# Reading out every other product of a seven-product matrix stage two clock steps later

## The chip, the cores and the metric

The kernel runs on one core of one Trainium2 chip. Its time is the device time of one execution in microseconds; three timed executions gave 789.0, 789.12 and 790.51, and the median, 789.12 us, is the time before. One more execution was profiled. That one took 790.67 us, of which 788.9 us are the span that the profiler shows, from the first to the last instruction. PE is TensorE (its matmuls; PEld are its weight loads), DVE is VectorE, ACT is ScalarE, POOL is GpSimd and SP issues the transfers.

## The reference, cut to what matters

One layer of a streaming encoder is computed for 512 prompt tokens and 64 sample tokens, 576 in all, with a model width of 1024 and a hidden width of 4096: an input projection, two kinds of attention, an output projection with a layer norm, a feed-forward part with a layer norm, and a gate. The change lies in the feed-forward part, in the product with `w_up`:

```python
hid = jnp.square(jax.nn.relu(jnp.einsum('bld,df->blf', x, w_up)))
x = layer_norm(ALPHA * x + jnp.einsum('blf,fd->bld', hid, w_down), ln2_g, ln2_b)
```

Everything is float32 in the reference.

## The kernel before, in words

**Precision.** Each float32 operand is held as two halves, a rounded high part and the rest (`BH`/`BL` for the layer's input, the two parts of a `whl` tile for a weight). One product of a weight block with an activation block is three matmuls: high times high, high times low, low times high. Weights arrive by DMA in `wraw` tiles; ACT casts the high part (line 183) and DVE subtracts it for the low part (line 187). The `whl` tiles form a ring, and a cast into one waits until PE has used what was in it.

**The feed-forward part.** The hidden width is cut into eight groups of 512. For each group there is an up stage, which fills `hid[g]`, and a down stage, which adds `hid[g]` times a block of `w_down` to `Y`. The order is U0, U1, D0, U2, D1, U3, ... D5, U7, and then the last two downs together with the second layer norm. `hid` has two buffers, `hidE` for even and `hidO` for odd groups, so a `hid[g]` is used a whole down stage after it has been filled.

**The seven-product stage.** U0 and U1 are plain. U2 to U7 (`up_sums`, lines 1319 to 1356) compute a two-by-two block product with seven block products in place of eight. Tokens are halved (A: 288, B: 288) and the width of 1024 is halved; sums of the weight blocks (line 210, into `wsum` or over `wraw`) and sums of the input blocks (`SX`, named `s` in the profile, made once ahead) feed the products. A group has two such pairs (`pair(0)` and `pair(1)`), each of seven products; a product is four width blocks times three matmuls, 12 matmuls of 128x128 by 128x288. So a stage has 2 x 7 x 12 = 168 matmuls, and a down stage has 8 x 2 x 12 = 192 of the same shape.

**Where products land.** PSUM has eight banks here: three tiles `g` of two banks each, used in turn (`psum_g`, line 1082), and two one-bank tiles `n` (`psum_n`). In a pair, products 0 and 1 go into the two banks of one `g` tile, 2 and 3 into those of the next, 4 and 5 into the third, and 6 into an `n` tile. Each product is then read out once or twice, by the short functions in `steps`:

- product 0: line 1330, ACT copies it to `u[0]`
- product 1: line 1331, DVE, `r[0] = ps + u[0]`
- product 2: line 1332, DVE, `u[1] = ps + u[0]`
- product 3: line 1333, DVE, `u[2] = ps + u[1]`
- product 4: line 1334, DVE, `r[1] = ps + u[2]`, and then `r[0:2]` goes through ReLU, square, cast and subtraction (lines 1349 to 1352) into `hid[g]`
- product 5: line 1335, DVE twice, `r[3]` and `r[2]`
- product 6: line 1336, DVE, `r[2]`, and then `r[2:4]` goes the same way into `hid[g]`

`u` has one buffer, `r` has two.

**What sets the order.** The kernel is written as a generator that yields after every six matmuls (`yield_every=6` in `gemm`, line 273), so a product is two steps. `drive` (line 89) advances `clock` by one at each yield, then runs up to three due entries of a queue. `later(delay, fn)` (line 71) puts `fn` into that queue, due at the clock of the call plus `delay`. A read-out with delay 0, put in after the second yield of its product, is thus written into the program after the first six matmuls of the next product. A scheduling layer then makes one stream of instructions for each engine out of what was written, in which it may let an instruction pass others that aren't ready, and puts semaphore waits where one engine needs another. On the chip each engine's stream runs in its order.

Of the kernel before, what the change touches and what calls it, by code (L numbers as in the profile page):

```python
# [10 lines left out]
AF = mybir.ActivationFunctionType  # L11
OP = mybir.AluOpType
# [24 lines left out]
def tile_hybrid_step(ctx: ExitStack, tc: tile.TileContext, I, O):  # L37
    nc = tc.nc
    PE, ACT, DVE, POOL, SP = nc.tensor, nc.scalar, nc.vector, nc.gpsimd, nc.sync
# [4 lines left out]
    def f(ap):  # L44
        return ap.bitcast(F32)
# [25 lines left out]
    def later(delay, fn):  # L71
        evq.append((clock[0] + delay, len(evq), fn))
# [200 lines left out]
    def gemm(ps, W, kmap, aH, aL, cols, yield_every=6, first=True, last=True, wc=slice(0, 128), k0=0):  # L273

        n = len(kmap) * 3
        i = 0
        for kw, ka in enumerate(kmap, k0):
            for w, a in ((0, aH), (0, aL), (1, aH)):
                PE.matmul(ps, W(w, kw, wc), a[:, ka, cols], start=(first and i == 0), stop=(last and i == n - 1))  # L279
                i += 1  # L280
                if i % yield_every == 0:
                    yield 1
# [799 lines left out]
    def psum_g():  # L1082
        turn[0] += 1
        if turn[0] % 3 == 2:
            return psB.tile([128, 2, 512], F32, name="g", tag="g", bufs=1)
        return psM.tile([128, 2, 512], F32, name="g", tag="m", bufs=2)

    def psum_n():
        return psN.tile([128, 512], F32, name="n", tag="n", bufs=2)
# [229 lines left out]
    def up_sums(g):  # L1319

        hid[g] = base.tile([128, 2, 4, NT], F32R, name="hidE", tag="AL") if g % 2 == 0 else \
            fb.tile([128, 2, 4, NT], F32R, name="hidO", tag="hidO")
        x11, x12, x22 = [[t[:, 4 * k:4 * k + 4, (A, B)[h]] for t in (BH, BL)] for h, k in ((0, 0), (0, 1), (1, 1))]
        def pair(m):
            h0 = WT.items[U["P", g, m]]["h0"]
            r = fs.tile([128, 4, HW], F32, name="r", bufs=2)
            u = fs.tile([128, 3, HW], F32, name="u")
            tt = DVE.tensor_tensor

            steps = ((x11, lambda ps: ACT.copy(u[:, 0], ps)),  # L1330
                     (x12, lambda ps: tt(r[:, 0], ps, u[:, 0], OP.add)),
                     (SX[2], lambda ps: tt(u[:, 1], ps, u[:, 0], OP.add)),  # L1332
                     (SX[3], lambda ps: tt(u[:, 2], ps, u[:, 1], OP.add)),
                     (x22, lambda ps: tt(r[:, 1], ps, u[:, 2], OP.add)),
                     (SX[1], lambda ps: (tt(r[:, 3], ps, u[:, 2], OP.subtract), tt(r[:, 2], ps, u[:, 1], OP.subtract))),
                     (SX[4], lambda ps: tt(r[:, 2], ps, r[:, 2], OP.add)))
            oh, ol = [hid[g][:, x, 2 * m:2 * m + 2].rearrange("p a (b t) -> p (a b) t", b=2) for x in range(2)]
            for i, (x, fn) in enumerate(steps):
                if i % 2 == 0:
                    G = psum_n()[:, None] if i == 6 else psum_g()  # L1340
                ps = G[:, i % 2, :HW]
                hv = WT.half(h0 + i)
                for _ in gemm(ps, lambda part, kw, wc, hv=hv: hv[part][:, kw, wc], range(4), x[0], x[1], slice(0, HW)):
                    WT.step()
                    yield 1
                later(0, lambda fn=fn, ps=ps: fn(ps))
                if i in (4, 6):
                    z = slice(i - 4, i - 2)
                    later(0, lambda z=z: ACT.activation(r[:, z], r[:, z], AF.Relu))
                    later(0, lambda z=z: ACT.activation(r[:, z], r[:, z], AF.Square))  # L1350
                    later(0, lambda z=z: ACT.copy(oh[:, z], r[:, z]))
                    later(0, lambda z=z: tt(ol[:, z], r[:, z], f(oh[:, z]), OP.subtract))

        WT.hold = True
        for m in range(2):
            yield from pair(m)
        WT.hold = False
# [208 lines left out]
```

## Time and profile before

| | |
|---|---|
| median of three executions | 789.12 us (789.0 to 790.51) |
| profiled execution | 790.67 us, span 788.9 us |
| PE busy | 779.4 us (99% of the span) |
| weight loads busy | 759.1 us (96%) |
| DVE, ACT, POOL busy | 540.9, 434.5, 119.0 us |
| six seven-product stages, U2 to U7 | 137.95 us together |
| six stages between and ahead of them, 192 matmuls each | 25.48 us each |

Matmuls overlap: one is shown for about 0.295 us and a new one starts about every 0.133 us. A busy PE therefore isn't a PE at its best pace, and the table's 99% hides short waits; what a wait costs is read from the distance between the starts. The feed-forward part with the changed lines runs from 414.16 us (start of U2) to 679.51 us (end of U7) after the span's start. Idle time of DVE and ACT costs nothing as long as PE doesn't wait for them.

### The profile page before, as it was taken

How to read it: one execution, taken by the hardware profiler on the slowest of the kernel's cores; microseconds unless marked ns; L12 is line 12 of the kernel's file. 1: busy time of each engine (PE TensorE's matmuls, PEld its weight loads, DVE VectorE, ACT ScalarE, POOL GpSimd, SP SyncE). 2: the span in 40 equal slices, each digit the busy share in tenths (PEclk: the TensorE clock that was granted, in tenths of full speed). 3: DMA queues.
4: the chain of work that ended last, by engine and by line, in shares of the span. 5: the costliest groups of instructions: out<-in, count | busy, mean ns of one | idle time of the engine just before them, and what ended most of it. 6: DMA issues, size and time to landing. Idle time of an engine off the chain costs nothing.

```text
span 788.9 us, 14810 instructions
## 1 busy us (share of the span) xinstructions
PE 779.4 (99%) x5822; PEld 759.1 (96%) x5822; DVE 540.9 (69%) x1100; ACT 434.5 (55%) x912; POOL 119.0 (15%) x121
## 2 busy tenths in 40 slices
PE   9999999999999999999999999999999999999997
PEld 8988899999999999999999999999999999999997
DVE  7578687897457465899747759476594865647553
ACT  5468666788877444686425437153462634616351
POOL 8102335354422000300000000000000000012200
PEclk9999999999999999999999999999999999999999
DMA  8637243263313224332304223051321413720001
GB/s 296 201 39 171 74 119 98 103 181 103 101 56 101 76 81 162 113 141 83 102 31 135 80 81 108 29 157 56 101 87 53 137 54 107 258 102 29 28 27 67
DMA packets 31126, 81.44 MB, mean 103 GB/s; under 512 B 5072, under 2 KB 10192, under 8 KB 30928
## 3 DMA queue, kind: packets, MB, share of 16 engines
q1 hardware_dynamic: 30768, 80.27, 32.9%
q8 instruction: 46, 0.75, 0.4%
q10 hardware_dynamic: 288, 0.22, 0.1%
q14 instruction: 24, 0.20, 0.1%
HBM read 66.38 MB, written 9.54 MB: 96 GB/s over the span
## 4 chain that ended last, share of the span: by engine, by line
PE 90%; DVE 5%; ACT 2%; issue 1%; DMA 1%; POOL 0%; DVEq 0%; SPq 0%; ACTq 0%
PE g L279 55%; PE m L279 20%; PE n L279 2%; PE T L65 2%; PE V L915 2%; DVE dbias L620 1%; PE S L829 1%; PE S L827 1%; PE X L65 1%; PE m L421 1%; PE m L428 1%; PE S L428 1%; DVE whl L187 1%; DMA xraw<-in_xT_dram 0%; DMA wraw<-in_w_up_dram 0%
## 5 line engine op out<-in xcount | busy, mean ns | idle before, releaser
L183 ACT CAST whl<-wraw 128x512 fp32r<-128x512 f32 (+1 forms) x226 | 134.8, 611 | 170.0 <-PE g L279 145.4
L279 PE MATMUL g<-BH,whl 128*128 128x288 f32 (+2 forms) x864 | 181.6, 297 | 0.5 <-DVE Y L1221 0.5
L279 PE MATMUL m<-AH,whl 128*128 128x288 f32 x736 | 177.7, 308 | 0.0
L187 DVE TENSOR_TENSOR whl<-wraw,whl 128x512 fp32r<-128x512 f32 (+1 forms) x192 | 129.7, 694 | 69.0 <-ACT whl L183 68.2
L279 PEld LDWEIGHTS g<-BH,whl 128*128 128x128 f32 x864 | 141.1, 188 | 2.7 <-ACT u L1330 1.2
L279 PEld LDWEIGHTS m<-AH,whl 128*128 128x128 f32 x736 | 126.3, 188 | 1.9 <-issue 1.0
L279 PE MATMUL g<-BL,whl 128*128 128x288 f32 (+2 forms) x432 | 127.3, 295 | 0.0
L279 PE MATMUL m<-AL,whl 128*128 128x288 f32 x368 | 109.0, 296 | 0.0
L279 PE MATMUL g<-hidE,whl 128*128 128x288 f32 (+2 forms) x768 | 103.4, 295 | 0.0
L279 PE MATMUL g<-hidO,whl 128*128 128x288 f32 (+2 forms) x768 | 103.3, 295 | 0.0
L279 PEld LDWEIGHTS g<-hidO,whl 128*128 128x128 f32 x768 | 102.3, 188 | 0.0
L279 PEld LDWEIGHTS g<-hidE,whl 128*128 128x128 f32 x768 | 102.2, 188 | 0.1
L279 PEld LDWEIGHTS g<-BL,whl 128*128 128x128 f32 x432 | 81.3, 188 | 0.2
L279 PEld LDWEIGHTS m<-AL,whl 128*128 128x128 f32 x368 | 69.5, 189 | 0.7
L279 PE MATMUL g<-s,whl 128*128 128x288 f32 x432 | 68.5, 298 | 0.0
L279 PEld LDWEIGHTS g<-s,whl 128*128 128x128 f32 x432 | 60.1, 188 | 2.2 <-DVE u L1332 1.1
L1111 POOL TENSOR_TENSOR ln_s<-Y 128x576 f32<-128x576 f32 (+2 forms) x3 | 4.4, 1463 | 381.7 <-DVE Y L1396 369.3
L187 POOL TENSOR_TENSOR whl<-wraw,whl 128x512 fp32r<-128x512 f32 x34 | 44.5, 1310 | 75.1 <-ACT whl L183 53.9
L845 ACT ACTIVATE sP<-sP,st 128x128 f32<-128x128 f32 (+4 forms) x72 | 39.6, 550 | 25.4 <-DVE st L837 25.0
L1371 DVE SCALAR_TENSOR_TENSOR Y<-Y,g 128x576 f32<-128x576 f32 x48 | 36.0, 750 | 21.7 <-PE g L279 21.2
L279 PE MATMUL m<-BH,whl 128*128 128x288 f32 x192 | 43.4, 304 | 0.0
L183 ACT CAST whl<-wsum 128x512 fp32r<-128x512 f32 x24 | 14.8, 616 | 33.0 <-PE g L279 32.8
(282 smaller groups left out, 1261.7 us busy)
## 6 DMA issues: line engine op xcount, KB each, us to landing
wraw<-in_w_up_dram SPq DMA_DIRECT2D x32, 512.0 KB, 3.5
wraw<-in_w_down_dram SPq DMA_DIRECT2D x32, 512.0 KB, 3.5
wraw<-in_w_qkv_dram SPq DMA_DIRECT2D x23, 512.0 KB, 3.7
wraw<-in_w_gate_dram SPq DMA_DIRECT2D x8, 512.0 KB, 4.4
wraw<-in_w_o_dram SPq DMA_DIRECT2D x8, 384.0 KB, 3.1
out_vT_dram<-v SPq DMA_DIRECT2D x8, 288.0 KB, 2.1
Y<-in_xT_dram SPq DMA_DIRECT2D x8, 288.0 KB, 4.7
PLD<-PL SPq DMA_DIRECT2D x4, 576.0 KB, 3.5
```

The source lines that it names most:

```text
L65: PE.transpose(out, in_, ident[:n, :n])
L183: ACT.copy(self.hv[h][0], src)
L187: eng.tensor_tensor(lv, src, f(hv), OP.subtract)
L279: PE.matmul(ps, W(w, kw, wc), a[:, ka, cols], start=(first and i == 0), stop=(last and i == n - 1))
L421: PE.matmul(mk[:, h, :HW], w0(part, k), a[:, k, h * HW:(h + 1) * HW], start=(k == 0 and i == 0), stop=(k == 7 and i == 2))
L428: PE.matmul(acc[b][:n[b], :304], a[:, k, b * 128:b * 128 + n[b]], ixw(part, k), start=(k == 0 and i == 0), stop=(k == 7 and i == 2))
L620: DVE.scalar_tensor_tensor(dst[:n, :nk], r[:n, :nk], w, dst[:n, :nk], op0=OP.mult, op1=OP.add)
L827: PE.matmul(ps[:, :n], Q[:, c], K[:, :n], start=True, stop=False)
L829: PE.matmul(ps[:, :n], Q[:, c], P["KL"][:, hh, :n], start=False, stop=True)
L845: ACT.activation(j["P"], j["P"], AF.Exp, bias=j["st"][:, 0:1], scale=-1.0, accum_out=s)
L915: PE.matmul(P["O"][r, (i - 1) * 128 + c.start:(i + 1) * 128], P["vt"][:, kb, r], t[:, hh, kb, c], start=(kb == 0), stop=(kb == i))
L1371: later(0, lambda y=y, m=m, s=s: DVE.scalar_tensor_tensor(y, y, s, m[:, :, :HW], op0=OP.mult, op1=OP.add))
```

## The change: the delay of three of the seven read-outs

In `pair`, the read-outs of products 0, 2 and 4, the first of each two-bank tile, are put into the queue with a delay of 2 in place of 0, and so are the four operations that follow the read-out of product 4. They are then written into the program after all twelve matmuls of products 1, 3 and 5 and no longer after the first six. The read-outs of products 1, 3, 5 and 6 keep delay 0. No operation is added or removed, and no tile or buffer count changes.

```diff
                 for _ in gemm(ps, lambda part, kw, wc, hv=hv: hv[part][:, kw, wc], range(4), x[0], x[1], slice(0, HW)):
                     WT.step()
                     yield 1
-                later(0, lambda fn=fn, ps=ps: fn(ps))
+                wait = 2 if i in (0, 2, 4) else 0
+                later(wait, lambda fn=fn, ps=ps: fn(ps))
                 if i in (4, 6):
                     z = slice(i - 4, i - 2)
-                    later(0, lambda z=z: ACT.activation(r[:, z], r[:, z], AF.Relu))
-                    later(0, lambda z=z: ACT.activation(r[:, z], r[:, z], AF.Square))
-                    later(0, lambda z=z: ACT.copy(oh[:, z], r[:, z]))
-                    later(0, lambda z=z: tt(ol[:, z], r[:, z], f(oh[:, z]), OP.subtract))
+                    later(wait, lambda z=z: ACT.activation(r[:, z], r[:, z], AF.Relu))
+                    later(wait, lambda z=z: ACT.activation(r[:, z], r[:, z], AF.Square))
+                    later(wait, lambda z=z: ACT.copy(oh[:, z], r[:, z]))
+                    later(wait, lambda z=z: tt(ol[:, z], r[:, z], f(oh[:, z]), OP.subtract))
```

The new line shifts all later lines by one: line 1349 before is 1350 after the change, and so on.

The order of the instructions moves on three engines, PE, ACT and DVE, and on them only between the start of U2 and the end of U7; the streams of SP and POOL are the same.

On **PE**, in the first pair of U2, from the middle of product 1 to the end of product 3. A row is a line, an operation, the tile written, the two tiles read, the size, and how often it stands there in a row; `g_5275` is the tile of products 0 and 1, `g_5307` that of products 2 and 3, `whl_4993` the weights of product 1, `whl_5015` those of product 2 and `whl_5036` those of product 3.

```order
-L279 MATMUL g_5275<-BH_1155,whl_4993 128x288
-L279 MATMUL g_5307<-s12_4749,whl_5015 128x288 x4
-L279 MATMUL g_5275<-BH_1155,whl_4993 128x288
+L279 MATMUL g_5275<-BH_1155,whl_4993 128x288 x2
 L279 MATMUL g_5275<-BL_1156,whl_4993 128x288
 L279 MATMUL g_5275<-BH_1155,whl_4993 128x288 x2
 L279 MATMUL g_5275<-BL_1156,whl_4993 128x288
 L279 MATMUL g_5275<-BH_1155,whl_4993 128x288
-L279 MATMUL g_5307<-s12_4749,whl_5015 128x288 x8
-L279 MATMUL g_5307<-s3_4750,whl_5036 128x288 x6
+L279 MATMUL g_5307<-s12_4749,whl_5015 128x288 x12
+L279 MATMUL g_5307<-s3_4750,whl_5036 128x288 x12
```

Before, product 1 was cut in two, and four matmuls of product 2 stood between its halves; product 3 was cut in two as well (the second half stood among the matmuls of product 4). Now each product's twelve matmuls stand together, in all twelve pairs.

On **DVE**, the same pair, from the read-out of product 1 (line 1331) to those of product 5 (line 1335). In brackets stand the engines and transfer queues for whose semaphores the instruction waits; the rows of line 187 make low parts of weights.

```order
-L1331 TENSOR_TENSOR r<-g,u 128x288 [waits PE_49,Activation_49]
+L1331 TENSOR_TENSOR r<-g,u 128x288 [waits Activation_49]
 L187 TENSOR_TENSOR whl<-wraw,whl 128x512 [waits DMAHW2_49,Activation_49]
 L187 TENSOR_TENSOR whl<-wraw,whl 128x512 [waits Activation_49]
 L1332 TENSOR_TENSOR u<-g,u 128x288 [waits PE_49]
-L1333 TENSOR_TENSOR u<-g,u 128x288 [waits DVE_49,PE_49]
+L1333 TENSOR_TENSOR u<-g,u 128x288 [waits DVE_49]
 L187 TENSOR_TENSOR whl<-wraw,whl 128x512 [waits DMAHW3_49,Activation_49]
 L187 TENSOR_TENSOR whl<-wraw,whl 128x512 [waits Activation_49]
 L1334 TENSOR_TENSOR r<-g,u 128x288 [waits DVE_49,PE_49]
-L1335 TENSOR_TENSOR r<-g,u 128x288 [waits PE_49]
```

The order is the same in this piece; the read-outs of products 1, 3 and 5 have lost their own wait for PE, since the read-out ahead of each now waits for the matmuls of both products of the tile.

On **ACT**, from the copy of product 0 in the first pair of U2 (line 1330) to that in the second. Before:

```order
L1330 COPY u<-g 128x288
L183 CAST whl<-wraw 128x512 x4
L1349 ACTIVATE r<-r 128x576
L1350 ACTIVATE r<-r 128x576
L183 CAST whl<-wraw 128x512
L1351 CAST hidE<-r 128x576
L183 CAST whl<-wraw 128x512 x2
L1349 ACTIVATE r<-r 128x576
L1330 COPY u<-g 128x288
```

With the change (1350, 1351 and 1352 are the former 1349, 1350 and 1351):

```order
L1330 COPY u<-g 128x288
L183 CAST whl<-wraw 128x512 x5
L1350 ACTIVATE r<-r 128x576
L1351 ACTIVATE r<-r 128x576
L183 CAST whl<-wraw 128x512
L1352 CAST hidE<-r 128x576
L1350 ACTIVATE r<-r 128x576
L183 CAST whl<-wraw 128x512
L1351 ACTIVATE r<-r 128x576
L1352 CAST hidE<-r 128x576
L1330 COPY u<-g 128x288
```

The copy of the second pair's product 0 now stands behind the whole second half of the first pair's activations; before, it stood ahead of the last two of them. One weight cast has moved ahead of the first ReLU.

## The prediction, as put on record before the run

> **What bounds the kernel now.** I read the page first, then the two kinds of stage side by side, then who makes PE wait, then one stall instruction by instruction. The page:
>
> ```profile
> span 788.9 us, 14810 instructions
> ...
> PE 779.4 (99%) x5822; PEld 759.1 (96%) x5822; DVE 540.9 (69%) x1100; ACT 434.5 (55%) x912; POOL 119.0 (15%) x121
> ...
> PE 90%; DVE 5%; ACT 2%; issue 1%; DMA 1%; POOL 0%; DVEq 0%; SPq 0%; ACTq 0%
> ```
>
> PE is the bound: 90% of the chain that ended last is its own work, and the other engines have room. Since matmuls overlap, 99% busy doesn't say that PE runs at its best pace. For that I cut the feed-forward part at the first matmul of each stage and compared the stages; first the six seven-product stages U2 to U7, then the six stages of 192 matmuls ahead of each of them (x counts matmuls that touch the window, so two from the stage before are among them; the column after the busy times is the granted clock):
>
> ```profile
> 414.16:437.18 23.02, 23.02 (x170) 22.37 (x169) 18.27 (x34) 13.72 (x25) 0.00 (x0) 1.00 0.44 138
> 462.66:485.59 22.93, 22.93 (x170) 22.38 (x169) 18.27 (x34) 13.73 (x25) 0.00 (x0) 1.00 0.46 138
> ...
> 656.30:679.51 23.21, 23.21 (x170) 22.43 (x169) 15.73 (x29) 13.33 (x24) 0.00 (x0) 1.00 0.48 148
> sum 137.95, PE 137.94 PEld 134.30 DVE 107.10 ACT 81.95 POOL 0.00; mean PE 22.99 PEld 22.38 DVE 17.85 ACT 13.66 POOL 0.00
> ...
> 437.18:462.66 25.48, 25.48 (x194) 25.48 (x193) 14.65 (x23) 7.79 (x13) 0.00 (x0) 1.00 0.15 42
> ...
> sum 152.89, PE 152.89 PEld 152.89 DVE 86.02 ACT 45.36 POOL 0.00; mean PE 25.48 PEld 25.48 DVE 14.34 ACT 7.56 POOL 0.00
> ```
>
> The reader is to see two things. The clock is 1.00 in both kinds, and the matmuls have one shape, yet the stages differ in pace: 25.48 / 192 = 0.1327 us from start to start between, and 22.99 / 168 = 0.1368 in the seven-product stages. And PEld, busy all of the time in the one kind, has holes in the other. At the pace of the others a seven-product stage would take 168 x 0.1327 = 22.295 us and the six 133.77; they take 137.95. **4.18 us** are lost in them. Who makes PE wait between 414 and 680 us:
>
> ```profile
> PEld g L279 <- ACT u L1330: 1.2, 6, 0.2
> PEld g L279 <- DVE u L1332: 1.1, 6, 0.2
> PEld g L279 <- DVE r L1334: 0.2, 1, 0.2
> ```
>
> These are the read-outs of products 0, 2 and 4 and nothing else: no weight tile (`whl`), no transfer. The first of these stalls in U2:
>
> ```profile
> 416.40 0.30 PE L279 MATMUL g<-BH,whl 128*128 128x288 f32 x1
> ...
> 416.54 0.69 PE L279 MATMUL g<-s,whl 128*128 128x288 f32 x4
> ...
> 416.73 0.40 ACT L1330 COPY u<-g 128x288 f32<-128x288 f32 x1 [0.17 <-PE g L279]
> 417.19 0.19 PEld L279 LDWEIGHTS g<-BH,whl 128*128 128x128 f32 x1 [0.19 <-ACT u L1330]
> 417.19 0.40 PE L279 MATMUL g<-BH,whl 128*128 128x288 f32 x1
> ...
> 417.42 0.29 PE L279 MATMUL g<-BL,whl 128*128 128x288 f32 x1
> ```
>
> Product 0 started at 414.16, so its twelfth matmul started at 414.16 + 11 x 0.1327 = 415.62. The copy that reads it began only at 416.73, 0.33 us after the start at 416.40 of the sixth matmul of product 1, which writes the tile's other bank. PE then had four matmuls of product 2 to do, and the second half of product 1 waited for the copy of product 0. So the program orders reads and writes by tile, not by bank: a read-out written between the halves of product 1 waits for the first half and holds up the second. The stall costs twice: the start at 417.19 comes 0.12 us after 416.54 + 4 x 0.133, and the one at 417.42 comes 0.10 late again because its weights weren't loaded ahead.
>
> [...]
>
> **The change, part by part.** Nothing is added or removed: as many matmuls, read-outs, transfers, and the streams of SP and POOL are unmoved.
>
> *The PE stream.* Each product's twelve matmuls now stand together, and each read-out of products 0, 2, 4 comes after the last write to its tile. No matmul is left behind a read-out of its own tile. What remains to wait for is a tile's slot, when the ring of three comes round, and weights; both are costed below. The pace then is that of the other stages. Two rows show that the operands don't matter for it: the plain U1 stage, with the operands `BH` and `BL`, and a run of 14 matmuls with the summed inputs `s`, which ends where the next row starts:
>
> ```profile
> 363.19:388.67 25.48, 25.48 (x194) 1.00 0.32 105
> ...
> 418.08 2.02 PE L279 MATMUL g<-s,whl 128*128 128x288 f32 x14
> 419.94 0.30 PE L279 MATMUL g<-BH,whl 128*128 128x288 f32 x1
> ```
>
> 25.48 / 192 again, and (419.94 - 418.08) / 14 = 0.133. So each of the six stages gives back all it lost: 0.73 in U2 (23.02 - 22.295), about 0.63 in each of U3 to U6, 0.92 in U7; **4.18 together**. It can't be more, since nothing faster than 0.1327 stands in any row of this shape; it is zero if the waits stay.
>
> *The later read-outs.* Their cost is worked from the first pair, with 0.33 us from the start of a last matmul to its reader. Rows of before, of DVE and, last, PE's first matmul of the second pair:
>
> ```profile
> 418.35 0.46 DVE L1331 TENSOR_TENSOR r<-g,u 128x288 f32<-128x288 f32 x1 [1.07 <-PE g L279]
> ...
> 420.67 0.45 DVE L1332 TENSOR_TENSOR u<-g,u 128x288 f32<-128x288 f32 x1
> 422.27 0.46 DVE L1333 TENSOR_TENSOR u<-g,u 128x288 f32<-128x288 f32 x1 [1.15 <-PE g L279]
> 422.96 1.29 DVE L187 TENSOR_TENSOR whl<-wraw,whl 128x512 fp32r<-128x512 f32 x2 [0.24 <-ACT whl L183]
> 424.18 0.45 DVE L1334 TENSOR_TENSOR r<-g,u 128x288 f32<-128x288 f32 x1
> 425.78 0.82 DVE L1335 TENSOR_TENSOR r<-g,u 128x288 f32<-128x288 f32 x2 [1.16 <-PE g L279]
> ...
> 425.99 0.29 PE L279 MATMUL g<-BH,whl 128*128 128x288 f32 x1
> ```
>
> Product 1's last matmul starts at 414.16 + 23 x 0.1327 = 417.21, so the copy of product 0 starts at 417.54, 0.81 later than the 416.73 of before, and ends at 417.94. Line 1331 follows at about 418.0, where it was at 418.35. Product 3's last starts at 420.40: line 1332 at 420.73 (was 420.67), 1333 at 421.2 (was 422.27). Product 5's last starts at 423.58: line 1334 behind the two rows of 187, 424.2 as before, and 1335 at 424.7 (was 425.78). Only the copy is later; the second reader of each tile, which frees it, is earlier, because its product is no longer cut in two.
>
> *The tiles' slots.* The first tile's slot is wanted by the second pair at 425.99 before and at 414.16 + 84 x 0.1327 = 425.31 after, and is free at about 418.5: 6.8 us to spare. Second tile: free at 421.7, wanted 24 matmuls later, at 428.5. Third: free at 425.5, wanted at 431.7, 6.2 to spare. Cost: nothing. Were that cover gone, each pair would pay what the copy comes later, 0.81 us.
>
> *Queued behind the copy.* ACT stands at line 1330 until product 1 ends, and behind it stand weight casts (in the second pair too, where the first pair's activations now all stand ahead of it). What hides the delay is the lead of the casts, which wait for PE to give buffers back (414 to 680 us):
>
> ```profile
> ACT whl L183 <- PE g L279: 131.0, 72, 5.0
> ```
>
> ACT is busy 13.73 of 22.93 us in a stage, so 9.2 are free for twice 0.81. DVE works 18.27 in a stage that shrinks to 22.3 (80% becomes 82%). Cost: nothing; with the cover gone again 0.81 for each of 12 pairs.
>
> *Downstream.* `hid[g]` is used a down stage later, and for U7 only after the first three units of U6's down; its last pieces end with the stage as before. The part behind U7 is wholly PE's on the chain and just starts 4.2 us earlier.
>
> **Sum.** Profiled execution: span 788.9 - 4.18 = 784.7, and with the 1.77 us outside the span (790.67 - 788.9) 786.5. That execution lies 1.55 above the median of the three runs shown, 789.12; from the median the sum is 789.12 - 4.18 = **784.9 us**, 0.53% less.
>
> **Rivals.**
>
> *Only the named waits go.* PEld's rows name 1.2 + 1.1 + 0.2 = 2.5 us; the other 1.7 of the 4.18 I put down to starts delayed by unloaded weights and small waits under the view's threshold. Should that part come from something else that stays, such as DVE's fuller queue, the time is 789.12 - 2.5 = 786.6. For it: the view names no more. Against: every long distance between starts in these stages sits at a cut product, as in the rows at 417.19 and 417.42.
>
> *The change doesn't do what it says.* If PE still waits for the same reads one place further on, the time stays 789.1. For it: the reads are as many, and a copy that frees a tile comes later. Against: the next matmul in the stream is in another tile.
>
> *Slots come back late.* Place: the first matmul into a reused tile; a copy that begins 0.81 us later holds the tile, PE waits in each of 12 pairs, 9.7 us, less the 4.18: 794.6. It decides from the point at which the 6 to 7 us to spare are used up. For it: DVE at 82% with in-order reads. Against: the second reader, not the copy, frees the tile, and it gets earlier. [...]
>
> **How the numbers follow.** Forecast (all of the 4.18) 0.80; named waits only 0.11; no effect 0.05; late slots 0.04. A measurement of this kernel tells 0.2%, 1.58 us, from no change: faster means under 787.54, slower over 790.70. The first two cases are faster (0.91), the third the same (0.05), the fourth slower (0.04). The range holds the first two cases: low 784.2, the forecast less half of the spread of 1.5 us among the runs before; high 787.0, the second rival with 0.4 of that spread, which is also the forecast with all of it and a little more. 0.09 of the chance lies outside by mechanism.
>
> **What would show it.** Right: six seven-product stages of 22.3 us each with PEld busy throughout, no PE row that names lines 1330, 1332 or 1334, the copy of product 0 about 0.8 us later after the stage's start, line 1331 about 0.35 earlier, the other stages at 25.48. Wrong: stages over 22.5; PEld waiting for a DVE row at the first matmul of a tile (slots), or for `whl` (casts behind the copy); or a later stage longer than before by what U2 to U7 gave.

## The result, and the profile after

The changed kernel takes 784.75 us (median of six executions, 784.2 to 786.21); before, measured beside it, took 790.52 (six executions, 789.0 to 790.64). The ratio is 0.9944 with a 95% interval of 0.9934 to 0.9954: faster by 0.56%, where 784.9 us and 0.53% had been forecast. The two medians alone would give 0.9927: four of the six executions before and two of the six after took about 1.5 us longer than the others, the late group below. The page of the changed kernel's profiled execution (784.64 us):

```profile
span 782.9 us, 14771 instructions
...
PE 772.8 (99%) x5822; PEld 756.4 (97%) x5822; DVE 539.9 (69%) x1100; ACT 434.2 (55%) x912; POOL 118.3 (15%) x121
...
PE 90%; DVE 4%; ACT 3%; DMA 1%; issue 1%; POOL 0%; SPq 0%; DVEq 0%; ACTq 0%
```

PE still bounds the kernel, with as many matmuls. The same stretches as before, cut at the first matmul of each stage (us; span, then busy time of PE, PEld, DVE, ACT and POOL, granted clock, transfers): U2, U7 and the sum of U2 to U7, then one of the stages between them and the sum of those six.

```profile
412.57:434.82 22.25, 22.25 (x170) 22.25 (x169) 18.76 (x35) 12.95 (x24) 0.00 (x0) 1.00 0.44 142
...
651.24:673.49 22.25, 22.25 (x170) 22.25 (x169) 16.64 (x30) 12.93 (x24) 0.00 (x0) 1.00 0.50 166
sum 133.52, PE 133.52 PEld 133.52 DVE 110.13 ACT 78.01 POOL 0.00; mean PE 22.25 PEld 22.25 DVE 18.35 ACT 13.00 POOL 0.00
...
434.82:460.31 25.48, 25.48 (x194) 25.48 (x193) 13.94 (x23) 8.46 (x14) 0.00 (x0) 1.00 0.14 42
...
sum 152.88, PE 152.88 PEld 152.88 DVE 82.55 ACT 48.66 POOL 0.00; mean PE 25.48 PEld 25.48 DVE 13.76 ACT 8.11 POOL 0.00
```

Each seven-product stage takes 22.25 us and PEld is now busy throughout, as in the other stages. The six went from 137.95 to 133.52, so **4.43 us** were gained there, and nothing in the stages between (152.89 and 152.88). From the end of U7 to the start of the kernel's last matmul both profiles show 104.68 us. No row of the view of waits names PE as waiting between 412 and 674 us any more; its longest waits are those of ACT and DVE for PE or for each other:

```profile
ACT whl L183 <- PE g L279: 134.3, 89, 5.0
DVE whl L187 <- ACT whl L183: 56.1, 47, 2.3
DVE Y L1372 <- PE g L279: 17.7, 15, 1.4
ACT u L1330 <- PE g L279: 5.8, 6, 1.0
```

The first pair of U2, the read-outs:

```profile
415.61 0.29 PE L279 MATMUL g<-BH,whl 128*128 128x288 f32 x1
...
415.74 2.01 PE L279 MATMUL g<-s,whl 128*128 128x288 f32 x14
415.94 0.40 ACT L1330 COPY u<-g 128x288 f32<-128x288 f32 x1 [0.96 <-PE g L279]
...
416.37 0.46 DVE L1331 TENSOR_TENSOR r<-g,u 128x288 f32<-128x288 f32 x1 [0.67 <-ACT u L1330]
...
419.11 0.46 DVE L1332 TENSOR_TENSOR u<-g,u 128x288 f32<-128x288 f32 x1 [0.18 <-PE g L279]
419.60 0.46 DVE L1333 TENSOR_TENSOR u<-g,u 128x288 f32<-128x288 f32 x1
...
422.30 0.46 DVE L1334 TENSOR_TENSOR r<-g,u 128x288 f32<-128x288 f32 x1 [0.19 <-PE g L279]
```

The copy of product 0 starts 0.33 us after product 1's last matmul, and PE is by then in product 2 and goes on.

**More than the stages in these two profiles.** The spans differ by 6.0 us, not 4.43. U2 starts 1.59 us earlier in the profile of after, ahead of any changed instruction, and that difference arises in the first 11 us, where the two kernels have the same streams. Matmuls there started 0.25 us apart until 10.49 in the profiled execution of before, and 0.13 to 0.14 apart from 5.48 on in that of after. Before:

```profile
9.98 0.46 PE L428 MATMUL m<-iw,AL 128*128 128x304 f32 x1
10.24 0.42 PE L428 MATMUL m<-iw,AH 128*128 128x304 f32 x1
10.49 0.31 PE L428 MATMUL S<-iw,AH 128*128 128x304 f32 x1
10.64 0.30 PE L428 MATMUL X<-iw,AH 128*128 128x304 f32 x1
```

The executions of both kernels fall into two groups some 1.5 us apart: 789.0 and 789.1 against 790.5 and 790.6 before, 784.2 to 784.8 against 786.2 after. Like against like, the difference is about 4.4 us (789.12 to 784.74, 790.61 to 786.2), which is what the stages gave. The experiments are therefore read from the sum of the six stages, which this doesn't touch.

### The profile page after: what moved, and what is told of

Same layout as the page of the kernel before. It is cut to its first block, busy times and chain, and to the rows that moved or that the text cites. A ratio compares the mean times of both kernels' runs of the same rounds, so it can differ in the third digit from the quotient of the medians.

```text
span 782.9 us, 14771 instructions
## 1 busy us (share of the span) xinstructions
PE 772.8 (99%) x5822; PEld 756.4 (97%) x5822; DVE 539.9 (69%) x1100; ACT 434.2 (55%) x912; POOL 118.3 (15%) x121
## 4 chain that ended last, share of the span: by engine, by line
PE 90%; DVE 4%; ACT 3%; DMA 1%; issue 1%; POOL 0%; SPq 0%; DVEq 0%; ACTq 0%
PE g L279 55%; PE m L279 20%; PE n L279 2%; PE T L65 2%; PE V L915 2%; PE S L829 1%; PE S L827 1%; PE X L65 1%; PE m L421 1%; PE m L428 1%; DVE whl L187 1%; PE S L428 1%; DVE dbias L620 1%; ACT work L615 1%; DMA kO<-kO 0%
## 5 line engine op out<-in xcount | busy, mean ns | idle before, releaser
L187 DVE TENSOR_TENSOR whl<-wraw,whl 128x512 fp32r<-128x512 f32 (+1 forms) x192 | 131.4, 696 | 77.3 <-ACT whl L183 76.7
L279 PE MATMUL g<-BH,whl 128*128 128x288 f32 (+2 forms) x864 | 178.2, 296 | 0.5 <-DVE Y L1221 0.5
L279 PE MATMUL g<-s,whl 128*128 128x288 f32 x432 | 61.1, 295 | 0.0
L279 PEld LDWEIGHTS g<-s,whl 128*128 128x128 f32 x432 | 58.5, 188 | 0.0
```

What stands on the lines that cost most here:

```text
L187: eng.tensor_tensor(lv, src, f(hv), OP.subtract)
```

## The experiments

The theory: PE lost time because the two banks of a tile are ordered as one, so that a product was cut in two and its second half waited for a read-out of the other bank. Rivals: the cut itself costs, or the order of tiles and weights that it brings; a read-out beside a write to another bank slows PE; and, against the change, later read-outs bring tiles back late.

### Product 0 alone, and products 2 and 4 alone

```diff
-                wait = 2 if i in (0, 2, 4) else 0
+                wait = 2 if i == 0 else 0
```

> Edit: only the read-out of product 0 keeps the delay of 2; those of products 2 and 4 are back at 0. The measure is the sum of the six seven-product stages: 137.95 us before, 133.52 with the whole change. Theory (each cut product costs what its own wait for a read-out costs): before, the starts around the read-out of product 0 were late by 0.23 us in a stage's first pair and by 0.08 in its second, 0.31 a stage, 1.9 in six; so 136.1. Rival (every cut costs alike, whoever is waited for): 4.43 / 36 cuts = 0.12 each, 12 of them gone, 1.5; so 136.5. Both: PE no longer waits for line 1330, and still waits for 1332 and 1334.

```diff
-                wait = 2 if i in (0, 2, 4) else 0
+                wait = 2 if i in (2, 4) else 0
```

> Edit: the read-outs of products 2 and 4 keep the delay of 2, that of product 0 is back at 0. Theory: the rest of the gain, 4.43 - 1.9 = 2.5, so the six stages take 135.4 us, and the gains of this kernel and of the one with product 0 alone add up to 4.43. Rival (every cut alike): 24 of 36 cuts gone, 2.95, so 135.0. If the two gains add up to clearly less than 4.43, the three waits cover for each other.

Measured: 136.38 us with product 0 alone and 136.20 with 2 and 4 alone (one execution each, 787.83 and 787.51). Who made PE wait, product 0 alone and then products 2 and 4 alone, each in the window of U2 to U7:

```profile
PEld g L279 <- DVE u L1332: 1.2, 6, 0.2
PEld g L279 <- DVE r L1334: 0.4, 2, 0.2
```

```profile
PEld g L279 <- ACT u L1330: 2.2, 12, 0.2
```

Each delay takes away the waits on its own line, as the theory has it; those that are left grow. So the sizes missed: 1.57 and 1.75 us gained, where 1.9 and 2.5 were expected, and together 3.32, not 4.43. The rival's numbers were 1.5, nearer to the first than the theory's, and 2.95, which missed the second by more. The last row shows why: with products 2 and 4 delayed, PE waits for the copy 12 times, in every pair, and only 6 times by that view before. The second pair of U2 in that kernel:

```profile
426.36 0.30 PE L279 MATMUL g<-BH,whl 128*128 128x288 f32 x1
...
426.50 1.35 PE L279 MATMUL g<-s,whl 128*128 128x288 f32 x9
...
426.77 0.68 ACT L1351 ACTIVATE r<-r 128x576 f32<-128x576 f32 x1
...
427.36 0.38 ACT L1330 COPY u<-g 128x288 f32<-128x288 f32 x1
...
427.79 0.40 PE L279 MATMUL g<-BH,whl 128*128 128x288 f32 x1
...
428.02 0.30 PE L279 MATMUL g<-BL,whl 128*128 128x288 f32 x1
```

The copy stands behind an activation and starts 1.00 us after product 1's sixth matmul (426.36); in the kernel before it was 0.74 us (428.96 after 428.22). The two starts behind the copy are late by 0.20 us together, where they were late by 0.08 before. So all twelve waits cost about the same, (136.20 - 133.52) / 12 = 0.22 us on average. A wait that was read as cheap in the old trace grew when the read-outs around it moved: the gains of the parts don't add up to that of the whole.

### A tile for each product, all delays 0

```diff
-                if i % 2 == 0:
-                    G = psum_n()[:, None] if i == 6 else psum_g()
-                ps = G[:, i % 2, :HW]
+                G = psum_n()[:, None] if i == 6 else psum_g()
+                ps = G[:, 0, :HW]
```

> Edit: the kernel before, all delays 0, but every product gets a two-bank tile of its own and uses its first bank alone, so that no read-out shares a tile with a later write. Read-outs come early, as before. Theory (the cost is the wait between two banks of one tile): no product is cut, the six stages take 133.5 us, the whole about 0.9944 of before, as with the change. Rival (reading one bank while PE writes another slows PE, or read-outs must come late): the stages stay near 137.9. Second rival (six tiles in place of three in a pair use up the ring): PE waits at the first matmul of a tile, stages over 134.

The ratio was 0.9947, interval 0.993 to 0.9964 (785.59 us, median of four, two of them some 1.5 us longer), and the six stages:

```profile
sum 133.52, PE 133.52 PEld 133.52 DVE 114.49 ACT 83.96 POOL 0.00; mean PE 22.25 PEld 22.25 DVE 19.08 ACT 13.99 POOL 0.00
```

The whole gain, to the hundredth, without any delay. The read-out comes early here, in the midst of product 1:

```profile
414.44 0.30 PE L279 MATMUL g<-BL,whl 128*128 128x288 f32 x1
...
414.51 0.40 ACT L1330 COPY u<-g 128x288 f32<-128x288 f32 x1 [0.96 <-PE g L279]
414.58 0.42 PE L279 MATMUL g<-BH,whl 128*128 128x288 f32 x2
```

ACT reads product 0 while PE writes product 1 to another bank, and the starts stay 0.13 us apart. So neither the early read-out nor reading beside writing cost anything here; the shared tile did. And six tiles to a pair in a ring of three brought no wait for a slot. This also parts the change's two sides: it isn't the later read that helps but that no write to the tile is left behind it.

### The cut without the wait

On top of the tile for each product, products 1 and 2, 3 and 4, 5 and 6 are interleaved by hand, six matmuls of each in turn. The middle of the edit (`...` stands for lines left out):

```diff
+                if i in (1, 3, 5):
...
+                    ps, g1 = product(i, hv)
+                    ahead[i + 1] = product(i + 1, WT.hv[h0 + i + 1])
+                    for gen in (g1, ahead[i + 1][1], g1):
+                        next(gen)
+                        WT.step()
+                        yield 1
...
```

> Edit: on top of the kernel with a tile for each product, products 1 and 2, 3 and 4, 5 and 6 are interleaved by hand, six matmuls of the one and six of the other in turn, as the order of before had them, but with nothing to wait for. Theory (a cut costs only by its wait): 133.5 us for the six stages. Rival (the cut itself costs, by the change of tile and weights in the middle of a product): about 137.9.

The chain of the first stage shows the order for products 5 (`g`) and 6 (`n`), pieces of six in turn (start, us, what); products 1 and 2, and 3 and 4, alternate in the same way from about 414.3 us on:

```profile
421.59 0.80 PE n L279 x6
422.38 0.79 PE g L279 x6
423.17 0.80 PE n L279 x6
423.97 8.81 PE g L279 x66
```

Six starts take 0.79 us, 0.132 each, and the six stages took 133.57 (one execution, 784.87 us). Cutting a product in two cost nothing here, to 0.05 us, where nothing waits; the rival of the costly cut is out.

### Fewer slots, and a longer read-out

```diff
-                    G = psum_n()[:, None] if i == 6 else psum_g()
+                    G = psum_n()[:, None] if i == 6 else psM.tile([128, 2, 512], F32, name="g", tag="m", bufs=2)
```

> Edit: the changed kernel, with a ring of two tiles for products 0 to 5 of a pair in place of three. Theory (slots have room): a tile is free 4.4 us after its first matmul (line 1331 ends at 416.83 in the changed kernel, the stage's first matmul is at 412.57, 0.1 for the handover) and wanted again after 48 matmuls, 6.36 us; 2.0 us to spare, so the six stages stay at 133.5 us. Rival (later read-outs bring the slots back late): stages over 134, PE waiting for line 1331, 1333 or 1335 at the first matmul of a tile.

```diff
-            steps = ((x11, lambda ps: ACT.copy(u[:, 0], ps)),
+            steps = ((x11, lambda ps: [ACT.copy(u[:, 0], ps) for _ in range(6)]),
```

> Edit: the changed kernel, ring of three, but the copy of product 0 is made six times over, so that product 0's read-out takes about 2 us longer and ACT has some 4 us more work in a stage. Theory (6.8 us to spare at the slot, ACT free for 9 us of a stage): the six stages stay at 133.5 us. Rival (what comes later on ACT is passed to PE through the slots or through late weight casts): up to 2 us in each of 12 pairs, some 24 us; stages toward 157.

The six stages, ring of two and then six copies (one execution each, 784.74 and 786.38 us; U2 starts at 412.66 us in the first and at 414.31 in the second):

```profile
sum 133.52, PE 133.52 PEld 133.52 DVE 109.50 ACT 78.23 POOL 0.00; mean PE 22.25 PEld 22.25 DVE 18.25 ACT 13.04 POOL 0.00
```

```profile
sum 133.52, PE 133.52 PEld 133.52 DVE 109.49 ACT 98.56 POOL 0.00; mean PE 22.25 PEld 22.25 DVE 18.25 ACT 16.43 POOL 0.00
```

Neither costs anything in the stages: a ring of two is enough, and ACT takes 3.4 us more work in a stage (16.43 against 13.00) unseen by PE. Then both together, with eight copies:

> Edit: both, a ring of two and the copy of product 0 made eight times. This looks for the point from which slots decide. A tile is then free about 4.4 + 7 x 0.35 = 6.9 us after its first matmul and wanted after 6.36: theory says that now PE does wait for line 1331 at tiles, some 0.5 us in each of 12 pairs, less what the scheduling layer puts in between: 134.5 to 140 us for the six stages. Rival (slots never decide in this range): 133.5.

```profile
PEld g L279 <- DVE r L1331: 4.3, 12, 0.6
```

```profile
422.32 0.29 PE L279 MATMUL n<-BH,whl 128*128 128x288 f32 x1
422.65 0.40 PE L279 MATMUL g<-BH,whl 128*128 128x288 f32 x1
422.89 0.29 PE L279 MATMUL g<-BL,whl 128*128 128x288 f32 x1
```

Here the slots decide. Line 1331, the second reader of the first tile, starts at 422.14 and takes 0.46; the next user of that slot, product 4, starts at 422.65, 0.20 later than the pace, and the start after it is late as well. PE waits once in each pair. The scheduling layer had put product 6 and three matmuls of the next pair ahead of that tile, so the stages can't be cut as before; from U2's first matmul to the kernel's last start it is 370.32 us against 365.60 with the change alone, 4.7 more, 0.39 a pair; with the 133.52 of the change that would be about 138.2 for the stages, within the forecast (one execution, 790.92 us, with U2's start at 414.12 us). The tile came free later than the 6.9 us of the forecast, 8.5 us after its first matmul (422.60 after 414.12), since weight casts stand between the copies on ACT. The rival of the late slots is a real mechanism with its price, but in these runs it shows only with two slots and a read-out some 4 us longer.

### Busy from the start

```diff
-WARM = 8
+WARM = 12
```

> Edit: the changed kernel with 12 in place of 8 idle matmuls of ones ahead of the first work (line 300), so that PE is busy from 1.06 to about 6.1 us without the hole of 0.4 us that it has now at 4.8. Question: executions of all kernels here fall into two groups 1.5 us apart (784.2 to 784.8 and 786.2 with the change), and in the profiled one of before matmuls start 0.25 us apart until 10.5 us, in the one of after 0.135 from 5.6 on. Theory (PE's clock comes up one step later where the early work has holes): the late group goes away or gets rarer, the median is 784.8 or less. Rival (it has nothing to do with the early matmuls): two groups as before, and up to 0.7 us lost where the added matmuls delay the first work.

Five executions gave 784.98 to 785.5, all in one group; nine of before beside them gave eight at 789.12 to 789.24 and one at 790.72. The ratio is 0.9947, interval 0.9933 to 0.996. The late group didn't show, and some 0.3 us were lost against the early group of the changed kernel (784.2 to 784.77; the median here is 785.07). With five executions, and one late in nine of before, the times point the theory's way but don't settle it, and it isn't a faster kernel than the changed one; the last section has what the traces add. The matmuls where the pace changes (first real work at 6.20):

```profile
6.59 0.38 PE L428 MATMUL m<-iw,AH 128*128 128x304 f32 x1
6.80 0.30 PE L428 MATMUL S<-iw,AH 128*128 128x304 f32 x1
7.09 0.40 PE L421 MATMUL m<-AL,whl 128*128 128x288 f32 x1
7.33 0.31 PE L428 MATMUL m<-iw,AL 128*128 128x304 f32 x1
7.47 0.30 PE L428 MATMUL S<-iw,AL 128*128 128x304 f32 x1
```

## Why the prediction was right, point by point

**What bounds.** Right: PE, and in the seven-product stages PE's waits for the read-outs of products 0, 2 and 4. All the rows that named them are gone, and the kernel with a tile for each product shows that the tie between the two banks of a tile was the cause.

**The size.** 4.18 us had been forecast for the stages, 4.43 came. The step that was off is the pace taken from the down stages, 0.1327 us: in these traces it is the pace of the stages with `hid` operands. Up stages run at 22.25 / 168 = 0.1325, and so did the plain U1 stage before, which the prediction cut 0.04 us too early for its check that operands don't matter. Cut at its first matmul it is

```profile
363.23:388.67 25.44, 25.44 (x194) 25.44 (x193) 22.77 (x33) 12.50 (x20) 0.00 (x0) 1.00 0.32 105
```

25.44 / 192 = 0.1325, and 6 x 168 x 0.1325 = 133.6 would have been nearly the 133.52. "It can't be more" was thus wrong by 0.25 us. Why a down stage's matmul takes 0.2% longer stays open.

**The later read-outs.** Worked after the stage's start, the copy of product 0 was put at 3.38 us and came at 3.37 (2.57 before), line 1331 at 3.84 (3.80), 1332 at 6.57 (6.54), 1333 at 7.04 (7.03). Line 1334 was expected behind two weight subtractions, at 10.04, and came at 9.73, as these had gone ahead. The second reader of the first tile did get earlier: line 1331 at 3.80, where it was at 4.19.

**Slots and queues.** Right: no wait for a slot and none for weights; a ring of two and a copy six times as long left the stages at 133.52, so the room was at least as large as reckoned. A later read-out cost PE nothing in these runs until the slots were used up: with two slots and eight copies it cost 0.39 us a pair.

**Rivals.** That only the 2.5 us of named waits would go is wrong: the distances between starts were the true measure, 4.43, and PEld's idle rows left out the second start that came late after most waits, and the small waits. The forecast's argument against this rival holds in all six stages of the profile before: every start over 0.02 us late against 0.1325 stands at a cut. In U3 they add up to 0.23, 0.22 and 0.16 us at the three cuts of the first pair and 0.08 at the first cut of the second; the other two cuts cost nothing there. No effect and late slots did not happen.

**The sum against the runs.** 784.9 forecast from a median of 789.12; the median of after is 784.75. The six runs of before have a median of 790.52, since more of them fell into the late group. That the forecast from the first median came within 0.15 us is in part luck, since both medians lie in the early group; the difference of the stages owes nothing to it. For the profiled execution a span of 784.7 had been forecast and 782.9 came: 0.25 us of that are the pace of the stages, and 1.59 the earlier start, which the sum took as unchanged.

## What to carry to other kernels

A tile that spans two banks may be ordered as one: a read of one bank that is written into the program between writes to the other cuts the writer's stream in two. Put the read behind the tile's last write, or give each accumulation its own tile; both gave all of the 4.43 us here. Measure what waits cost by the distance between starts against a clean stretch of the same operands, not by the idle time that the view names (2.5 of 4.43 us here), and don't add up what single parts of a change will give.

## What the runs showed of the hardware beside this

Before, after and the kernel with a tile for each product have executions some 1.5 us longer than their others; the five with 12 idle matmuls don't. In the profile of before, matmuls of 288 to 304 columns start about 0.25 us apart up to 10.24 us and 0.13 to 0.15 from 10.49 on; in that of after from 5.48 on, but around a wait of 0.90 us that ends at 7.10. The granted clock in the rows stands at 1.00 in both (before, then after):

```profile
7.00:10.50 3.50, 3.40 (x14) 3.37 (x15) 3.43 (x6) 2.50 (x7) 1.91 (x3) 1.00 1.00 348
```

```profile
7.00:10.50 3.50, 3.40 (x25) 3.39 (x26) 3.46 (x6) 1.70 (x4) 1.98 (x3) 1.00 0.95 323
```

14 matmuls against 25 in the same 3.5 us: here that column doesn't tell the pace, the distance between starts does. The view shows 1.00 wherever the trace holds no record of the clock, and the first record, of the full clock, begins at 10.49 us in the trace of before and at 4.57 in that of after. In the kernel with a ring of two and eight copies the column does show a slow stretch, 14 matmuls in 3.20 us at 0.50 and then 25 in 3.10 at 1.00:

```profile
7.50:10.70 3.20, 3.20 (x14) 3.17 (x14) 3.09 (x6) 2.34 (x6) 1.49 (x2) 0.50 0.98 345
10.90:14.00 3.10, 3.10 (x25) 3.08 (x24) 2.58 (x3) 2.64 (x7) 3.10 (x6) 1.00 1.06 411
```

PE idles ahead of its first real matmul at 5.27 us in both profiles, 0.43 us before and 0.50 after, so in these two that hole doesn't tell the late start from the early one. With 12 idle matmuls PE is busy for all of the 4.00 us from 4 to 8. That holes in the early work bring the late group stays the author's estimate; what sets the moment of the change of pace was not shown.
